# Modulating x and context by pairs of channel chunks, with a new order of loads and products and unread products while x arrives

## The chip, the cores and the metric

The kernel runs on one core of a Trainium2 chip. The metric is the device time of one execution in microseconds. Before the change it is 1221.16 us, the median of three runs (1216.76, 1221.16 and 1223.71). The engines are named as the profile names them: PE (TensorE, with PEld for its weight loads), ACT (ScalarE), DVE (VectorE), POOL (GpSimd) and SP (SyncE, which here only issues DMAs).

## The reference, cut to what matters

One layer of a trunk with three token mixers and a mixture of experts. The change touches only what stands in front of the mixers: the normalised input is scaled and shifted per channel ("modulated") and multiplied by the columns of `w_in`. x has 512 tokens, the context 256, and both have 1024 channels.

```python
def rms_norm(x, g):                      # float32: x * rsqrt(mean(x*x) + EPS) * g
def modulate(h, shift, scale):
    return h * (1 + scale[:, None, :]) + shift[:, None, :]
# shift, scale = columns 0..1023 and 1024..2047 of  silu(c) @ w_mod + b_mod
# (c for x, c_ctx for the context);  h = rms_norm(x, g_mix)
px = split_columns(hx @ w_in)            # hx: modulated x, hc: modulated context
pc = split_columns(hc @ w_in)            # retention, window, neighbourhood attention, gates follow
...
# router, 16 experts of 64 tokens each, final norm
```

## The kernel before

Tokens are turned so that channels lie on the 128 partitions; there are eight chunks `k` of 128 channels. A modulated chunk is kept as two float32r tiles, a rounded part ("hi", `hx0h`) and the rest ("lo", `hx0l`; a tile `hx0` holds chunks 0 and 1, `hx1` holds 2 and 3, and so on; `hc0` and `hc1` hold four context chunks each). A product with 128 columns of `w_in` is three matmuls on each chunk: hi by hi, hi by lo, lo by hi (`quantum`). A "unit" is one such product over all eight chunks, and a pump (`Pump`) runs the many units of the kernel one after another between the mixers' own work.

`start()` builds the modulated chunks and runs the first two units meanwhile: those of v and k of the first retention head. Their weights come as tiles `rw` and are split by `halves` into `wv` and `wk`. Their sums for x lie in the PSUM banks `px` and `om`, those for the context in two banks named `oc`. For each chunk these steps follow one another:

- `load_mod(k)`: two DMAs of 512 KB of `w_mod` into `wm` (128 columns of shift and 128 of scale for all 1024 channels of c, so 512 bytes to a piece).
- `mod_rows`: 16 matmuls on 32 columns of PE each give shift and scale as rows; ACT copies them to `rm`.
- `mod_cols`: two matmuls with `rm` as weights turn them into columns; DVE adds the bias (`modT`) and makes the factor (`am`).
- `turn_x`, `turn_c`: PE transposes of the normalised rows `xs` (four tiles of x, two of the context) into one of the rotating PSUM banks `pa`.
- `modulate`: ACT writes hi, then DVE (for the context ACT) the full value `tf`, then DVE subtracts for lo.
- `prod`: the three matmuls of both units, for x (512 columns) and for the context (256).

`row_stat` has ACT square each row tile (`junk`) with a sum, and DVE and POOL make the factor `rstd` of it; `row_norm` applies it on DVE. `pinned[0] = True` holds every engine to the order in which `start()` is written. In that order the rows of chunk k+2, the columns and the modulation of chunk k+1 and the products of chunk k stand beside one another. SP issues DMAs in program order, each on one of eight semaphores, so a DMA waits for the landing of the eighth before it. Behind `start()` the units and the mixers follow, then routing, then 16 experts whose weights (201 MB) are streamed through the buffers that come free.

Of the kernel before, what the change touches and what calls it, by code (L numbers as in the profile page):

```python
# [8 lines left out]
F32 = mybir.dt.float32  # L9
# [40 lines left out]
def kernel(ctx, tc, x, c, cctx_x, c_ctx, w_mod, b_mod, g_mix, g_ffn, w_in, decay, ret_gn, w_ret,  # L50
# [74 lines left out]

    def split(hi, lo, src):
        A.activation(hi, src, AF.Copy)
        V.tensor_tensor(lo, src, f32(hi), op=OP.subtract)
# [15 lines left out]
            [(sink_b, dap(sink, 0, [[0, P], [1, HW]]))]]  # L144
    xs = []
    for i in range(4):
        xs.append(Tp.tile([P, D], F32, name="xs", tag="t"))
        SY.dma_start(xs[i], dap(x, i * P * D, [[D, P], [1, D]]))
        for dst, src in vecs[i]:
            SY.dma_start(dst, src)  # L150
    ident = cs[:, C_ID:C_ID + P]
# [49 lines left out]
    NM = 6 * D  # L201
# [25 lines left out]
    def load_mod(k):  # L227
        ts = []
        for part in range(2):
            t = Tp.tile([P, KT, P], F32, name="wm", tag="t")  # L230
            SY.dma_start(t, dap(w_mod, part * D + k * P, [[NM, P], [P * NM, KT], [1, P]]))  # L231
            ts.append(t)
        return ts

    def mod_rows(wt):
        o = px()
        for part in range(2):
            for k2 in range(2):
# [7 lines left out]
    def mod_cols(k, rm):  # L246
        o = px()
        for j in range(2):
            mm(o[:, 2 * j:2 * j + 2], rm[:, j * P:(j + 1) * P], sel2, True, True)
        b_ = colv[:, 16:32].rearrange("p (a k) -> p a k", a=2)[:, :, k:k + 1]  # L250
        V.tensor_tensor(modT[:, :, k, :], o[:, 0:4].rearrange("p (a n) -> p a n", a=2), b_.to_broadcast([P, 2, 2]),
                        op=OP.add)
        V.tensor_scalar(am[:, k, :], modT[:, 1, k, :], 1.0, colv[:, 32 + k:33 + k], op0=OP.add, op1=OP.mult)
# [7 lines left out]
    def turn_c(k):  # L261
        o = pa()
        for t in range(2):
            PE.transpose(o[:, t * P:(t + 1) * P], xs[4 + t][:, k * P:(k + 1) * P], ident)
        return o[:, :CTX]
# [434 lines left out]
    def start():  # L700
        us = [r0[0], r0[2]]
        wm = [load_mod(0)]
        raw = [us[0].load()]
# [4 lines left out]
        raw.append(us[1].load())  # L708
        wm.append(load_mod(2))
        wm.append(load_mod(3))  # L710
# [14 lines left out]
        def mod_x(k, o):  # L725
            modulate(HX(k), HX(k, 1), o, k, 0)

        def mod_c(k, o):
            modulate(HC(k), HC(k, 1), o, k, 1)
# [3 lines left out]
        for i in (0, 2):  # L733
            row_stat(i, i + 2)
            row_norm(i, i + 2, 0)
        ox, oc, rm = {}, {}, {}
        wsp = []

# [6 lines left out]
        def rows_of(k):  # L745
            rm[k] = mod_rows(wm[k])
            if k < 4:
                wm.append(load_mod(k + 4))

        rows_of(0)  # L750
        ox[0] = turn_x(0)
        if HV == 0:
            wsp.append(halves(raw[0], "wv", V))
        mod_cols(0, rm[0])
        if HV == 1:
            wsp.append(halves(raw[0], "wv", V))
        mod_x(0, ox[0])
        ox[1] = turn_x(1)
        if HV == 2:
            wsp.append(halves(raw[0], "wv", V))  # L760
        rows_of(1)
        mod_cols(1, rm[1])
        prod(0, 0, c=False)
        mod_x(1, ox[1])
        wsp.append(halves(raw[1], "wk", G))
        row_stat(4, 6)
        prod(0, 1, c=False)
        row_norm(4, 6, 0)
        rows_of(2)
        prod(1, 0, c=False)  # L770
        mod_cols(2, rm[2])
        ox[2] = turn_x(2)
        prod(1, 1, c=False)
        oc[0] = turn_c(0)
        mod_c(0, oc[0])
        mod_x(2, ox[2])
        oc[1] = turn_c(1)
        mod_c(1, oc[1])
        rows_of(3)
        for i in range(2):  # L780
            prod(i, 0, x=False)
        oc[2] = turn_c(2)
        mod_c(2, oc[2])
        for i in range(2):
            prod(i, 1, x=False)
        ox[3] = turn_x(3)
        row_norm(0, 6, 1)
        rope_table(0)
        pump.prime()
        for k in range(2, KT):  # L790
            tick(T0)
            if k < 7:
                mod_cols(k + 1, rm[k + 1])
                tick(T1)
                mod_x(k + 1, ox[k + 1])
                tick(T2)
            for i in range(2):
                prod(i, k, c=False)
            if k < 7:
                oc[k + 1] = turn_c(k + 1)  # L800
                mod_c(k + 1, oc[k + 1])
                tick(T3)
            if k < 6:
                rows_of(k + 2)
            for i in range(2):
                prod(i, k, x=False)
            if k < 6:
                ox[k + 2] = turn_x(k + 2)
            if k == 5:
# [934 lines left out]
```

## Time and profile before

| | us |
|---|---|
| runs | 1216.76, 1221.16, 1223.71 |
| profiled execution | 1221.08 |
| its span, first to last instruction | 1219.3 |
| PE busy | 1155.5 (95% of the span) |
| DVE busy | 617.3 (51%) |
| ACT busy | 403.9 (33%) |

The page's chain of work that ended last is 62% PE and 25% DMA (the experts' weights), 7% DVE. A page of the profile shows busy shares over the whole span; what `start()` costs is read from the timeline of its first 70 us. A row of the timeline begins with the start and the duration in us; in square brackets stands how long the engine was idle before it and what it was released by.

### The profile page before, as it was taken

Reading aid. Unit: us, or ns where it says so; the run is one execution under the profiler, and the core shown is the slowest. Engines: PE = TensorE matmul, PEld = TensorE weight load, DVE = VectorE, ACT = ScalarE, POOL = GpSimd, SP = SyncE. Lnnn points to the kernel's source line nnn. Section 1 sums busy time; section 2 is a strip of 40 time slices with the busy share of each in tenths; the row PEclk is TensorE's granted clock in tenths of the full one; section 3 lists DMA queues with packets and bytes.
Section 4 is the critical chain, followed back from the end, with each engine's and each line's share of the span. In section 5 each row is a group of like instructions: output and inputs, shape, how many; then the busy total and the mean of one; then the engine's idle time right before and its main releaser. Section 6 shows DMA issues by size and latency. Waiting matters only on the chain.

```text
span 1219.3 us, 15848 instructions
## 1 busy us (share of the span) xinstructions
PE 1155.5 (95%) x5876; PEld 714.0 (59%) x5876; DVE 617.3 (51%) x1380; ACT 403.9 (33%) x779; POOL 87.0 (7%) x150
## 2 busy tenths in 40 slices
PE   4999999999999999999999979999999999999995
PEld 2788888777668887788888744333333323233322
DVE  3687666698867664677646352232332223222213
ACT  4544334576645553232332232112111111111112
POOL 1011211100040220000000000000000000000001
PEclk9999999999999999999999979999999999999998
DMA  9822112111012124887637548999999999999994
GB/s 274 219 87 70 52 52 89 53 36 35 19 52 62 35 61 166 291 268 244 206 103 293 207 173 313 405 409 409 409 409 409 409 409 409 409 409 409 409 409 184
DMA packets 159978, 285.57 MB, mean 234 GB/s; under 512 B 10838, under 2 KB 100250, under 8 KB 159900
## 3 DMA queue, kind: packets, MB, share of 16 engines
q1 hardware_dynamic: 158172, 278.27, 62.6%
q0 software_dynamic: 1152, 4.19, 0.9%
q10 hardware_dynamic: 576, 2.10, 0.4%
q8 instruction: 46, 0.75, 0.3%
q14 instruction: 32, 0.26, 0.1%
HBM read 280.33 MB, written 4.19 MB: 233 GB/s over the span
## 4 chain that ended last, share of the span: by engine, by line
PE 62%; DMA 25%; DVE 7%; ACT 2%; SPq 1%; issue 1%; POOL 1%; DVEq 0%; POOLq 0%; ACTq 0%
PE px L119 26%; DMA rg<-in_w_exp_up_dram 16%; PE pa L67 10%; PE px L67 8%; DMA rg<-in_w_exp_down_dram 8%; PE pa L119 7%; PE PV L119 3%; PE oc L119 3%; PE pa L1041 1%; PE pa L955 1%; DVE ws L295 1%; PE oy L119 1%; DMA wm<-in_w_mod_dram 1%; DVE rt L445 1%; SPq L231 1%
## 5 line engine op out<-in xcount | busy, mean ns | idle before, releaser
L67 PE MATMUL pa<-rg,xe 128*64 128x512 f32 x1024 | 264.5, 609 | 7.3 <-DMA rg<-in_w_exp_up_dram 4.9
L67 PEld LDWEIGHTS pa<-rg,xe 128*64 128x64 f32 x1024 | 72.4, 137 | 155.4 <-issue 108.7
L67 PE MATMUL px<-rg,hid 128*64 128x512 f32 x512 | 120.2, 601 | 10.9 <-DMA rg<-in_w_exp_down_dram 10.2
L295 DVE TENSOR_TENSOR ws<-rw,ws 128x1024 fp32r<-128x1024 f32 x55 | 68.8, 1252 | 55.6 <-PE px L119 34.9
L67 PEld LDWEIGHTS px<-rg,hid 128*64 128x64 f32 x512 | 32.8, 136 | 90.3 <-issue 48.5
L119 PE MATMUL px<-hx0h,ws 128*128 128x512 f32 x224 | 83.3, 401 | 0.0
L119 PE MATMUL px<-hx3h,ws 128*128 128x512 f32 x224 | 83.2, 398 | 0.0
L119 PE MATMUL px<-hx2h,ws 128*128 128x512 f32 x224 | 82.7, 397 | 0.0
L119 PE MATMUL px<-hx1h,ws 128*128 128x512 f32 x224 | 82.6, 398 | 0.0
L67 DVE SCALAR_TENSOR_TENSOR tt<-px,gcol,m 128x512 f32<-128x512 f32 x16 | 12.0, 751 | 127.7 <-PE px L67 127.7
L67 ACT ACTIVATE yy<-tt 64x512 fp32r<-64x512 f32 x32 | 20.1, 628 | 144.6 <-DVE tt L67 144.2
L67 DVE TENSOR_TENSOR acc<-px,acc 128x512 f32<-128x512 f32 x58 | 37.5, 687 | 59.3 <-PE px L67 59.3
L119 PE MATMUL px<-yh,ws 128*128 128x512 f32 x192 | 62.3, 390 | 0.8 <-ACT mod L1165 0.8
L294 ACT ACTIVATE ws<-rw 128x1024 fp32r<-128x1024 f32 x55 | 57.8, 1052 | 6.4 <-DMA rw<-in_w_in_dram 5.9
L911 ACT ACTIVATE Sx<-Sx,nm 128x512 f32<-128x512 f32 (+1 forms) x64 | 47.9, 748 | 34.7 <-DVE nm L947 19.5
L1160 DVE SCALAR_TENSOR_TENSOR mac<-mw,cpad,mac 128x1024 f32<-128x1024 f32 x30 | 38.5, 1283 | 18.9 <-DMA mw<-in_w_mod_dram 16.6
L119 PEld LDWEIGHTS px<-hx3h,ws 128*128 128x128 f32 x224 | 42.1, 189 | 7.9 <-issue 1.1
L119 PEld LDWEIGHTS px<-hx0h,ws 128*128 128x128 f32 x224 | 42.2, 189 | 7.7 <-issue 0.7
L119 PEld LDWEIGHTS px<-hx2h,ws 128*128 128x128 f32 x224 | 42.6, 190 | 7.1 <-issue 0.2
L119 PEld LDWEIGHTS px<-hx1h,ws 128*128 128x128 f32 x224 | 42.2, 188 | 7.2
L67 ACT ACTIVATE gu<-pa 128x512 f32<-128x512 f32 x16 | 9.5, 596 | 110.1 <-PE pa L67 110.1
L67 DVE TENSOR_SCALAR xe<-px,af,sf 128x128 f32<-128x128 f32 (+1 forms) x36 | 14.0, 403 | 61.1 <-ACT xe L67 41.8
(432 smaller groups left out, 2158.2 us busy)
## 6 DMA issues: line engine op xcount, KB each, us to landing
rg<-in_w_exp_gate_dram SPq DMA_DIRECT2D x128, 512.0 KB, 10.2
rg<-in_w_exp_up_dram SPq DMA_DIRECT2D x128, 512.0 KB, 10.2
rg<-in_w_exp_down_dram SPq DMA_DIRECT2D x128, 512.0 KB, 10.2
rw<-in_w_in_dram SPq DMA_DIRECT2D x58, 512.0 KB, 3.8
mw<-in_w_mod_dram SPq DMA_DIRECT2D x32, 512.0 KB, 4.8
wm<-in_w_mod_dram SPq DMA_DIRECT2D x16, 512.0 KB, 7.4
rw<-in_w_out_dram SPq DMA_DIRECT2D x8, 512.0 KB, 3.6
xs<-in_x_dram SPq DMA_DIRECT2D x4, 512.0 KB, 4.2
```

The costliest lines, as they stand in the source:

```text
L67: return (lambda *a_, **k_: tc.keep_in_program_order(f(*a_, **k_))) if pinned[0] else f
L119: PE.matmul(o, lhsT, rhs, start=start, stop=stop)
L231: SY.dma_start(t, dap(w_mod, part * D + k * P, [[NM, P], [P * NM, KT], [1, P]]))
L294: A.activation(hi, raw, AF.Copy)
L295: V.tensor_tensor(lo[:, :NV], raw[:, :NV], f32(hi[:, :NV]), op=OP.subtract)
L445: V.tensor_copy(t2[b:b + q], o[c:c + q])
L911: A.activation(Sx[:, :n], Sx[:, :n], AF.Exp, scale=-1.0, bias=nm, accum_out=l[:, 0:1])
L955: PE.transpose(o[:, j * P:(j + 1) * P], SXs[b, j][:, ti * P:(ti + 1) * P], ident)
L1041: PE.transpose(o[:, b * P:(b + 1) * P], SXs[a, b][:, ti * P:(ti + 1) * P], ident)
L1160: V.scalar_tensor_tensor(macs[w], tiles[i], cpad[:, k, 0:1], macs[w], op0=OP.mult, op1=OP.add)
```

## The change

- `load_mod(j)` loads the shift and scale of two chunks at once: four DMAs of 512 KB, 256 columns each (1 KB to a piece). The first four are issued right behind x, then both units' weights (`rw`), then the next four, then the context, then the last eight as their buffers come free.
- `mod_rows` and `mod_cols` work on pairs: 16 matmuls of 256 columns, then four with `rm`.
- Columns, modulation and products of a pair follow its rows directly. The context's first two pairs are both modulated in the round of the second x pair.
- The context's statistics and the rest of the normalisation stand ahead of the loop over pairs; the lo part of `wk` is made by DVE instead of POOL.
- `Warm`: eleven matmuls whose result nothing reads: for each tile of x one of 8 columns that reads the tile, and two of 256 columns on constants; two more behind the first pair's columns. They write the bank of the first unit, whose first real product starts it anew.

```diff
+    class Warm:
+        def __call__(self, dep=None, n=1):
+            if dep is not None:
+                k = dep.shape[0]
+                mm(self.o[:, :dep.shape[1]], ident[0:k, :], dep, True, True)
+            for _ in range(n):
+                mm(self.o[:, 0:256], ident, cs[:, 0:256], True, True)
...
+    def load_mod(j):
+        ts = []
+        for part in range(2):
+            for h in range(2):
+                t = Tp.tile([P, 4, 256], F32, name="wm", tag="t")
+                SY.dma_start(t, dap(w_mod, 4 * h * P * NM + part * D + j * 256, [[NM, P], [P * NM, 4], [1, 256]]))
+                ts.append(t)
+        return ts
...
     def mod_rows(wt):
...
                 for g in range(4):
-                    mm(o[32 * g:32 * g + 32, P * part:P * part + P], cpad[:, 4 * k2 + g, :],
-                       wt[part][:, 4 * k2 + g, :], k2 == 0, k2 == 1)
-        rm = h2(name="rm", shape=(P, 2 * P))
-        A.activation(rm, o[:, 0:2 * P], AF.Copy)
+                    mm(o[32 * g:32 * g + 32, 256 * part:256 * part + 256], cpad[:, 4 * h + g, :], wt[2 * part + h][:, g, :],
+                       h == 0, h == 1)
+        rm = h2(name="rm")
+        A.activation(rm, o, AF.Copy)
...
+        warm = Warm(om[0][0])
+        for i in range(4):
+            warm(xs[i][:, 0:8], 2)
         for i in (0, 2):
             row_stat(i, i + 2)
             row_norm(i, i + 2, 0)
...
+        rm = mod_rows(wm[0])
+        wm.append(load_mod(2))
+        ox[0], ox[1] = turn_x(0), turn_x(1)
+        mod_cols(0, rm)
+        wsp.append(halves(raw[0], "wv", V))
+        warm(n=2)
+        mod_x(0)
         prod(0, 0, c=False)
+        mod_x(1)
+        wsp.append(halves(raw[1], "wk", V))
+        prod(0, 1, c=False)
+        ox[2] = turn_x(2)
+        prod(1, 0, c=False)
+        prod(1, 1, c=False)
+        ox[3] = turn_x(3)
+        row_norm(0, 4, 1)
         row_stat(4, 6)
         row_norm(4, 6, 0)
+        row_norm(4, 6, 1)
+        for j in range(1, 4):
+            k = 2 * j
+            rm = mod_rows(wm[j])
+            if j == 1:
+                wm.append(load_mod(3))
+            if j == 2:
+                rope_table(0)
+                pump.prime()
+            mod_cols(j, rm)
+            mod_x(k)
+            kc = 0 if j == 1 else k
+            oc[kc], oc[kc + 1] = turn_c(kc)
+            prod(0, k, c=False)
+            prod(1, k, c=False)
+            mod_x(k + 1)
+            if j < 3:
                 ox[k + 2] = turn_x(k + 2)
+            prod(0, k + 1, c=False)
+            prod(1, k + 1, c=False)
+            while kc <= k:
+                for i_ in range(2):
+                    mod_c(kc + i_)
+                    tick(2)
...
+                for i_ in range(2):
+                    for i in range(2):
+                        prod(i, kc + i_, x=False)
+                kc += 2
+                if kc <= k:
+                    oc[kc], oc[kc + 1] = turn_c(kc)
+            if j < 3:
+                ox[k + 3] = turn_x(k + 3)
+            tick(6)
```

How the instructions stand now. In the PE's row before, in the middle of the loop, stand the rows of chunk 5 (`px<-wm,cpad`), the context's products of chunk 3 (`oc<-`), x turned for chunk 5 (`pa<-cs,xs`), the columns of chunk 5 (`px<-cs,rm`) and the first x product of chunk 4 (`hx2h`):

```order
L67 MATMUL px<-wm,cpad 32x128 x16
L67 MATMUL oc<-hc0h,wv 128x256
L67 MATMUL oc<-hc0l,wv 128x256
L67 MATMUL oc<-hc0h,wv 128x256
L67 MATMUL oc<-hc0h,wk 128x256
L67 MATMUL oc<-hc0l,wk 128x256
L67 MATMUL oc<-hc0h,wk 128x256
L67 MATMUL pa<-cs,xs 128x128 x4
L67 MATMUL px<-cs,rm 128x2 x2
L67 MATMUL px<-hx2h,wv 128x512
```

Now, in the round of chunks 4 and 5, the rows, the columns, the turned context and the x products that need them follow one another:

```order
L67 MATMUL px<-wm,cpad 32x256 x16
L67 MATMUL px<-cs,rm 128x2 x4
L67 MATMUL pa<-cs,xs 128x128 x4
L67 MATMUL px<-hx2h,wv 128x512
L67 MATMUL px<-hx2l,wv 128x512
L67 MATMUL px<-hx2h,wv 128x512
```

So the work that stood between a chunk's rows, its columns and its products has moved behind them.

On ACT, around the context's two squares (`junk`), the row before has the copy of a chunk's rows behind them and then context and x chunks in turn, and two copies of rows (`rm`) ahead:

```order
L67 ACTIVATE rm<-px 128x256
L67 ACTIVATE hx0h<-pa,modT,am 128x512
L67 ACTIVATE wk<-rw 128x512 x2
L67 ACTIVATE junk,ssq<-xs 128x1024 x2
L67 ACTIVATE rm<-px 128x256
```

Now the second pair's copy `rm` stands behind the squares, and both its chunks (`hx1h`) behind it:

```order
L67 ACTIVATE hx0h<-pa,modT,am 128x512 x2
L67 ACTIVATE wk<-rw 128x512 x2
L67 ACTIVATE junk,ssq<-xs 128x1024 x2
L67 ACTIVATE rm<-px 128x512
L67 ACTIVATE hx1h<-pa,modT,am 128x512 x2
```

So ACT reaches chunks 2 and 3 of x only when the context has landed and been squared; before, context chunk 0 and x chunk 2 stood there. On SP the loads stood in this order behind x:

```order
L231 DMA wm<-in_w_mod_dram 128x8x128 x2
L289 DMA rw<-in_w_in_dram 128x8x128
L231 DMA wm<-in_w_mod_dram 128x8x128 x2
L707 DMA xs<-in_ctx_dram 128x1024 x2
L289 DMA rw<-in_w_in_dram 128x8x128
L231 DMA wm<-in_w_mod_dram 128x8x128 x12
```

and now in this:

```order
L165 DMA wm<-in_w_mod_dram 128x4x256 x4
L309 DMA rw<-in_w_in_dram 128x8x128 x2
L165 DMA wm<-in_w_mod_dram 128x4x256 x4
L727 DMA xs<-in_ctx_dram 128x1024 x2
L165 DMA wm<-in_w_mod_dram 128x4x256 x8
```

The context has moved from behind five DMAs of 512 KB (without x) to behind ten. Behind the first retention head all five engines have the same instructions in the same order as before.

## Rows read from the trace of the kernel before

**Rows 1.** Windows: span of each stretch, busy us by engine, granted clock, DMA share, GB/s.
```profile
20.00:40.00 20.00, 16.99 (x144) 11.83 (x136) 8.89 (x22) 9.45 (x18) 4.05 (x4) 1.00 1.08 300
40.00:60.00 20.00, 19.36 (x227) 16.32 (x226) 15.10 (x52) 10.84 (x20) 0.00 (x0) 1.00 0.76 194
60.00:110.00 50.00, 49.26 (x250) 40.51 (x249) 38.26 (x72) 22.31 (x34) 8.59 (x9) 1.00 0.26 74
720.00:740.00 20.00, 17.70 (x70) 10.23 (x72) 6.29 (x32) 3.50 (x12) 1.22 (x1) 0.56 0.33 113
780.00:800.00 20.00, 20.00 (x96) 7.44 (x94) 6.45 (x14) 3.80 (x7) 0.00 (x0) 1.00 1.03 409
```

**Rows 2.** Timeline of PE in `start()`: start, us, what, [idle before, releaser].
```profile
31.26 0.63 PE L67 MATMUL om<-hx0l,wk 128*128 128x512 f32 x1
31.69 0.63 PE L67 MATMUL om<-hx0h,wk 128*128 128x512 f32 x1
...
40.63 0.40 PE L67 MATMUL px<-hx1l,wv 128*128 128x512 f32 x1
40.86 0.39 PE L67 MATMUL px<-hx1h,wv 128*128 128x512 f32 x1
```

**Rows 3.** Timeline of PE, two rounds of the loop at full rate.
```profile
44.72 0.63 PE L67 MATMUL pa<-cs,xs 128*128 128x128 f32 x4 [0.64 <-DVE tf L67]
45.18 0.51 PE L67 MATMUL px<-cs,rm 128*128 128x2 f32 x4
...
54.00 0.51 PE L67 MATMUL px<-cs,rm 128*128 128x2 f32 x4
```

**Rows 4.** Windows with source L119: the pump's matmuls up to the end of `start()`.
```profile
61.00:67.55 6.55, 4.66 (x19) 1.00 0.82 241
```

**Rows 5.** Timeline of PE and ACT where `start()` first uses a landed load.
```profile
14.40 1.08 PE L67 MATMUL px<-wm,cpad 128*32 128x128 f32 x16 [4.22 <-DVE xs L67]
...
26.28 1.15 ACT L67 ACTIVATE wk<-rw 128x512 fp32r<-128x512 f32 x2 [1.24 <-DMA rw<-in_w_in_dram]
```

**Rows 6.** DMA totals, of 35 to 41 us and of 800 to 860 us.
```profile
DMA packets 3445, 1.75 MB, mean 291 GB/s; under 512 B 52, under 2 KB 3444, under 8 KB 3444
```
```profile
DMA packets 6733, 24.55 MB, mean 409 GB/s; under 512 B 748, under 2 KB 748, under 8 KB 6730
```

**Rows 7.** Timeline, the context's statistics: the second square and the first normalisation.
```profile
28.38 1.04 ACT L67 ACTIVATE junk<-xs 128x1024 f32<-128x1024 f32 x1
...
31.58 0.88 DVE L67 TENSOR_SCALAR xs<-xs,rstd 128x512 f32<-128x512 f32 x2
```

**Rows 8.** Timeline, from a chunk's columns to its product with lo.
```profile
22.74 1.02 PE L67 MATMUL px<-cs,rm 128*128 128x2 f32 x4 [0.51 <-ACT rm L67]
...
24.26 0.78 ACT L67 ACTIVATE hx0h<-pa,modT,am 128x512 fp32r<-128x512 f32 x1 [1.57 <-DVE am L67]
...
25.07 0.81 DVE L67 TENSOR_SCALAR tf<-pa,am,modT 128x512 f32<-128x512 f32 x1 [0.85 <-ACT hx0h L67]
...
25.92 0.69 DVE L67 TENSOR_TENSOR hx0l<-tf,hx0h 128x512 fp32r<-128x512 f32 x1
...
26.66 0.80 PE L67 MATMUL px<-hx0l,wv 128*128 128x512 f32 x1 [0.78 <-DVE hx0l L67]
```

**Rows 9.** Timeline at full rate: rows, their copy, a context chunk, a copy of 512 columns.
```profile
47.32 1.08 PE L67 MATMUL px<-wm,cpad 128*32 128x128 f32 x32
...
47.48 0.56 ACT L67 ACTIVATE hc1h<-pa,modT,am 128x256 fp32r<-128x256 f32 x1
...
48.53 0.39 ACT L67 ACTIVATE rm<-px 128x256 f32<-128x256 f32 x1
...
66.69 0.58 ACT L477 ACTIVATE vt<-px 128x512 f32<-128x512 f32 x1
```

**Rows 10.** Windows: PE empty, and PE just after it had work again.
```profile
232.50:235.40 2.90, 0.00 (x0) 0.00 (x0) 2.83 (x5) 1.26 (x2) 1.22 (x1) 1.00 0.00 0
236.00:239.00 3.00, 3.00 (x11) 2.52 (x10) 2.77 (x8) 1.47 (x3) 0.00 (x0) 0.50 0.58 171
```

More of the change, by code (lines that the diff above doesn't have):

```diff
@@ L150 @@
             SY.dma_start(dst, src)
+    wmod0.append(load_mod(0))
     ident = cs[:, C_ID:C_ID + P]
@@ L225, in row_norm @@
             E.tensor_scalar(v, v, rstd[:, i:i + 1], None, op0=OP.mult)
[L227 to L233, printed above, removed]
     def mod_rows(wt):
@@ L237, in mod_rows, with mod_cols @@
         for part in range(2):
-            for k2 in range(2):
+            for h in range(2):
                 for g in range(4):
-                    mm(o[32 * g:32 * g + 32, P * part:P * part + P], cpad[:, 4 * k2 + g, :],
-                       wt[part][:, 4 * k2 + g, :], k2 == 0, k2 == 1)
-        rm = h2(name="rm", shape=(P, 2 * P))
-        A.activation(rm, o[:, 0:2 * P], AF.Copy)
+                    mm(o[32 * g:32 * g + 32, 256 * part:256 * part + 256], cpad[:, 4 * h + g, :], wt[2 * part + h][:, g, :],
+                       h == 0, h == 1)
+        rm = h2(name="rm")
+        A.activation(rm, o, AF.Copy)
         return rm
-    def mod_cols(k, rm):
+    def mod_cols(j, rm):
         o = px()
[L248 to L253, printed above, removed]
+        for c_ in range(4):
+            mm(o[:, 2 * c_:2 * c_ + 2], rm[:, c_ * P:(c_ + 1) * P], sel2, True, True)
+        ks = slice(2 * j, 2 * j + 2)
+        b_ = colv[:, 16:32].rearrange("p (a k) -> p a k", a=2)[:, :, ks]
+        V.tensor_tensor(modT[:, :, ks, :], o[:, 0:8].rearrange("p (a k n) -> p a k n", a=2, n=2),
+                        b_[:, :, :, None].to_broadcast([P, 2, 2, 2]), op=OP.add)
+        V.scalar_tensor_tensor(am[:, ks, :], modT[:, 1, ks, :], 1.0,
+                               colv[:, 32 + 2 * j:34 + 2 * j][:, :, None].to_broadcast([P, 2, 2]), op0=OP.add, op1=OP.mult)
     def turn_x(k):
@@ L262, in turn_c @@
         o = pa()
-        for t in range(2):
-            PE.transpose(o[:, t * P:(t + 1) * P], xs[4 + t][:, k * P:(k + 1) * P], ident)
-        return o[:, :CTX]
+        for i in range(2):
+            for t in range(2):
+                PE.transpose(o[:, i * CTX + t * P:i * CTX + (t + 1) * P], xs[4 + t][:, (k + i) * P:(k + i + 1) * P], ident)
+        return o[:, :CTX], o[:, CTX:]
     def modulate(hi, lo, o, k, who):
@@ L701, in start @@
         us = [r0[0], r0[2]]
-        wm = [load_mod(0)]
-        raw = [us[0].load()]
+        wm = wmod0
+        raw = [u.load() for u in us]
         wm.append(load_mod(1))
@@ L723, in prod, with mod_x, mod_c @@
             us[i].quantum(k % 4, w, om[i][0] if x else None, om[i][1] if c else None, k=k)
[L725 to L729, printed above, removed]
+        def mod_x(k):
+            modulate(HX(k), HX(k, 1), ox.pop(k), k, 0)
+        def mod_c(k):
+            modulate(HC(k), HC(k, 1), oc.pop(k), k, 1)
         om = [(px(), OC()[:, :CTX]), (pa("om"), pa("oc")[:, :CTX])]
         pinned[0] = True
[L733 to L737, printed above, removed]
         dg = decays()
@@ L743, in tick @@
                 next(dg, None)
[L745 to L761, printed above, removed]
@@ L774, in start @@
[L774 to L807, printed above, removed]
-                ox[k + 2] = turn_x(k + 2)
-            if k == 5:
-                pump.prime2()
+        row_norm(4, 6, 1)
@@ new lines, in start @@
+        for j in range(1, 4):
[14 more added lines that the diff above has]
+            if j < 3:
+                ox[k + 2] = turn_x(k + 2)
+            prod(0, k + 1, c=False)
[4 more added lines that the diff above has]
+                    tick(2)
+                if j == 3:
+                    pump.prime2()
+                for i_ in range(2):
+                    for i in range(2):
+                        prod(i, kc + i_, x=False)
[5 more added lines that the diff above has]
+            tick(6)
```

21 lines of the change are left out of this document (8 added, 13 removed).

## Prediction

> **What bounds the kernel now.** I read the windows first. Between 20 and 110 us PE is busy 16.99 of 20, 19.36 of 20 and 49.26 of 50 us [rows 1], so from about 40 us on a microsecond of delay in `start()` is a microsecond for PE, and the mixers behind it are PE's too. The experts' loads do not swallow it: from 780 us on they run at 409 GB/s, but from 720 to 740 us at 113 GB/s [rows 1], with their buffers full until PE uses the first of them; their long run begins when PE gets there. I therefore count a shift at the end of `start()` in full.
>
> The timeline of PE in `start()` gives its two speeds. At 31 us two matmuls of 512 columns start 0.43 us apart, at 40 us 0.23 us apart [rows 2]: half rate (1.2 GHz) and full rate (2.4 GHz). The change in speed lies between, at about 34 us. The rounds of the loop at full rate show how tight the present order is: from the columns at 45.18 to those at 54.00 two chunks pass, 4.41 us each, with one wait of 0.64 us just ahead [rows 3]. The last product of `start()` ends at about 67.5 us, but 19 matmuls of the pump stand among its last ones [rows 4]; at 0.23 us they are 4.3 us. Without them `start()` ends at 63.2 us. That is the number to beat.
>
> **The change, step by step.** I give times on the axis of the profile of before, and add up what PE waits for in its new row.
>
> *The loads.* Before, PE uses the first `wm` tile at 14.4 us, and ACT gets the second unit's weights, seven DMAs later, at 26.28 [rows 5]: 7 x 0.524 MB in 11.9 us, 308 GB/s. Those pieces are of 512 bytes (291 GB/s when nothing else runs); pieces of 4 KB run at 409 [rows 6]. For the 1 KB pieces of the new `wm` tiles no row stands alone, so their rate lies between 291 and 409; I take the middle, 350, or 1.5 us for a DMA, with 1.7 for `rw` and 1.3 for the context. In the new order the context ends eleven DMAs behind the first `wm`: 7 x 1.5 + 2 x 1.7 + 2 x 1.3 = 16.5, so at 14.3 + 16.5 = 30.8 us. The ends are 14.3 + 11 x 1.28 = 28.4 and 14.3 + 11 x 1.80 = 34.1.
>
> The Trainium skill ("DMA: Bandwidth & Descriptors", section "Why small descriptors are slow") puts a fixed overhead of about three beats of 32 bytes on each packet. By that estimate 1 KB gains 9% on 512 bytes, not 20%, and the context would land about a microsecond later; no row here shows it.
>
> *Up to the rows of the second pair.* The unread matmuls fill PE while x lands, and I let them lift it to full rate before the first `wm` is used, instead of at 34 us. This buys little by itself, for what follows waits for loads and for ACT and DVE. The first pair's last `wm` lands at 14.3 + 3 x 1.5 = 18.8, `rw` at 20.5; ACT splits it in 1.15 [rows 5] and makes hi in 0.8 [rows 8], to 22.5; DVE is then still at the second of two subtractions of 0.69, to 23.0, and gives a lo every 1.5 (0.81 + 0.69 [rows 8]), the second at 26.1. Behind it PE has the rest of chunk 1, a turned chunk, six matmuls of the second unit and a turned chunk, 2.9, to 29; the second pair's rows end at 30.8.
>
> *The context's statistics ahead of the second pair.* ACT copies the second pair's rows only behind both squares, DVE adds its bias only behind the context's normalisation. From the start of the second square to the first normalisation pass 3.2 us, and a pair of normalisations takes 0.88 [rows 7]; there are two pairs. So 30.8 + 3.2 + 1.8 = 35.8 us until DVE reaches the second pair. From the end of the columns (23.76) to ACT's hi (24.26) pass 0.5 us, from there to the product with lo (26.66) 2.4 [rows 8]. PE goes on at 35.8 + 0.5 + 2.4 = 38.7 us. Since 30.8 it has had only some columns and one turned pair to do. Before, at this time, it has done nearly the same work (the x products of two chunks, the context's of one or two, the rows of four). So up to here the change gains and loses nothing.
>
> *The three rounds.* What a round adds is the line rows, copy, columns, modulation, in which PE now has nothing else to do. At full rate, for a pair: the rows take 1.8 us (32 records of 128 columns take 1.08, twice the columns somewhat less than twice that); the copy of 512 columns 0.13 + 0.58 [rows 9]; four column matmuls 0.85 (two take 0.51 with their tail [rows 3]); then 0.5 and 2.4 as above. That is 6.3 us until lo is there. The rest: five matmuls at 0.23, 1.1; a turned chunk 0.5 (0.63 with its tail [rows 3]); six matmuls of the second chunk 1.4 (its lo is ready 1.5 after the first's, just in time); the context's twelve of 256 columns, at half of 0.23, 1.4; a turned chunk 0.5: 4.9. A round takes 11.2 us where two chunks took 8.8.
>
> - The round of chunks 2 and 3, from 38.7: 4.3 for x and the first context pair; then the second context pair, which is turned and modulated with PE waiting: 0.5, four ACT operations of 0.56 [rows 9] less overlap and a subtraction 2.5, the last matmuls 0.6, a turned chunk 0.5. To 47.1.
> - The round of chunks 4 and 5: 11.2, to 58.3.
> - The round of chunks 6 and 7, without turned chunks: 6.3 + 1.1 + 0.3 + 1.4 + 1.4 = 10.5, to 68.8.
>
> Against 63.2 this is 5.6 us later, at full rate throughout.
>
> *The clock.* PE has 8 us nearly without work before 38.7. A stall of 2.9 us with nothing in it was followed by a granted clock of 0.50 while PE worked through (236 to 239 us) [rows 10], a wait of 0.64 us was not [rows 3]. So full rate is lost there; the row shows 3 us of work at half, I take 4 with its edges, which cost 2 us. The rounds of chunks 4 and 5 and of 6 and 7 have each a wait of 0.7 us and, since the turned context needs a bank that DVE's `tf` frees, one of 2.1 us (0.5 + 0.78 + 0.81). The nearer row, 2.9, says that the rate falls; I take it for one of the two rounds, 2 us, and keep 0 and 4 as ends.
>
> *What moves out of `start()`.* The pump's first splits of weights now stand behind DVE's work for the two units; before, three stood ahead. PE has 11 us of pump work per two units there, so I take 0.5 us (0 to 2.4, two subtractions of 1.2). The `wk` lo on DVE instead of POOL, and SP's later loads (rope, the pump's weights), lie inside the waits above.
>
> Sum: 5.6 + 2 + 2 + 0.5 = 10 us. The durations are of the profiled execution, 1221.08 us (span 1219.3 and 1.8 around it), which is within 0.1 us of the median of the runs. Forecast: 1231 us, 0.8% slower.
>
> **Rivals.**
>
> *The clock holds.* If the waits in the later rounds and the one at 30 us do not cost full rate, or the columns and turned chunks in them keep it up, only 5.6 us and less remain; with the context at 28.4 us instead of 30.8 it is 3 us. For it speaks that waits of half a microsecond are harmless; against it rows 10. 1224 to 1227 us.
>
> *Faster: PE at full rate from 15 us is what counts.* Of PE's 17 us of work between 20 and 40 us [rows 1] the most runs at half rate, which the unread matmuls could spare. If PE's waits in the rounds were covered, the loads alone would set the end: the last `wm` lands 15 x 1.5 + 3.4 + 2.6 = 28.5 us after the first, at 42.8; the last pair needs 9.3 us more, so 52.1, 11 us ahead of 63.2, 1210 us. It decides at one point: whether the x products of chunk 2 run by about 32 us. Against it stand the rows of ACT, in which the copy waits for the context, and of PE, in which no other products stand between a pair's rows and its modulation.
>
> *Much slower: each wait costs the clock.* The Trainium skill ("TensorE: Matmul & The Clock Gate", section "HAM oscillation") describes bursts of matmuls with waits between, each of which starts at half rate anew. As a mechanism here: the fall at 30 us, both later rounds, and the second context pair's wait, 2 us each, with the context at 34.1: 5.6 + 8 + 3.3 + 0.5 = 17 us, 1238 us. No row shows the clock behind a wait of about 2 us.
>
> *The unread products do nothing.* If they do not lift the rate, the rows of the second pair end some 2 us later than the context's statistics allow; it adds at most 2 us to the forecast, and stays inside it.
>
> **The numbers.** The forecast with its neighbours (7 to 14 us slower, the fourth rival in it) gets 0.53, the holding clock 0.26, the much slower case 0.12, the faster 0.09. A difference under 0.5% (6 us) can hardly be told from none in this kernel, whose runs of before lie 7 us apart. Slower by more than that: nearly all of the forecast, the much slower case and little of the holding clock, 0.66; within it 0.25; faster 0.09. The range leaves out the faster case and the worst: 1220 to 1239 us.
>
> **What would show it.** Right: the first 512-column matmuls near 22 us 0.23 us apart; PE nearly idle between 31 and 38 us, put down to ACT and DVE; its granted clock 0.50, or matmuls 0.43 apart, just behind it; rounds of about 11 us; the first pump matmul near 70 us; the rest shifted by the same amount. Wrong: the x products of chunk 2 before 34 us, rounds under 9.5 us, or a shift at 70 us that is gone at 230.

## The result and the profile after

| | median of runs, us | ratio to before (95% interval) | span of the profiled run, us |
|---|---|---|---|
| before | 1221.08 (1216.76 to 1223.71, 4 runs) | | 1219.3 |
| after | 1231.89 (1231.48 to 1238.55, 4 runs) | 1.0119 (1.0098 to 1.0141) | 1229.7 |

The change makes the kernel slower, as forecast, and the median is 0.9 us from the forecast time. The ratio, 1.2%, is not the quotient of the two medians, which is 0.9% (10.8 us): the one run of 1238.55 weighs in it. The time is lost where the prediction looked for it. The first four stretches of [rows 1], the last moved by 11 us since the work in it is (busy us of PE, PEld, DVE, ACT and POOL, granted clock, DMA share, GB/s):

```profile
20.00:40.00 20.00, 13.69 (x80) 9.20 (x79) 12.60 (x29) 9.69 (x17) 1.54 (x2) 0.81 1.09 354
40.00:60.00 20.00, 15.95 (x103) 12.48 (x103) 9.03 (x36) 6.01 (x12) 0.00 (x0) 0.85 0.47 129
60.00:110.00 50.00, 46.60 (x255) 37.73 (x254) 32.51 (x52) 22.83 (x34) 5.15 (x5) 0.97 0.22 64
731.00:751.00 20.00, 16.16 (x72) 9.15 (x74) 7.71 (x37) 4.70 (x14) 1.22 (x1) 0.63 0.32 114
```

PE is busy 3.3 us less from 20 to 40 us, 3.4 less from 40 to 60 and 2.7 less behind that, and the granted clock is below 1.00 in all three. The 1.00 of before in the first stretch is not full rate throughout: up to about 34 us its products of 512 columns start 0.43 us apart [rows 2], while the window shows 1.00 from the first microsecond on. That early in a run the spacing tells the clock, not the window. The loads are faster (354 GB/s where they ran at 300) and over sooner (129 GB/s in the second stretch), which helps little: none of PE's waits below is put down to a load, and one of ACT's is (1.08 us for the context).

The timeline of PE in `start()` shows the waits; its line has start, length, the operation and, in brackets, the idle time before it and what ended it:

```profile
22.17 0.50 PE L67 MATMUL px<-hx0h,wv 128*128 128x512 f32 x1 [0.36 <-ACT hx0h L67]
...
29.91 1.93 PE L67 MATMUL px<-wm,cpad 128*32 128x256 f32 x32
33.16 1.05 PE L67 MATMUL px<-cs,rm 128*128 128x2 f32 x8 [1.31 <-ACT rm L67]
35.24 1.26 PE L67 MATMUL pa<-cs,xs 128*128 128x128 f32 x4 [1.03 <-DVE xs L67]
37.51 0.80 PE L67 MATMUL px<-hx1h,wv 128*128 128x512 f32 x1 [1.00 <-ACT hx1h L67]
39.08 0.80 PE L67 MATMUL px<-hx1l,wv 128*128 128x512 f32 x1 [0.78 <-DVE hx1l L67]
...
49.61 1.93 PE L67 MATMUL px<-wm,cpad 128*32 128x256 f32 x32
52.26 1.05 PE L67 MATMUL px<-cs,rm 128*128 128x2 f32 x8 [0.72 <-ACT rm L67]
55.43 0.66 PE L67 MATMUL pa<-cs,xs 128*128 128x128 f32 x4 [2.11 <-DVE tf L67]
...
62.80 1.93 PE L67 MATMUL px<-wm,cpad 128*32 128x256 f32 x32
65.45 1.05 PE L67 MATMUL px<-cs,rm 128*128 128x2 f32 x8 [0.72 <-ACT rm L67]
68.71 0.63 PE L67 MATMUL pa<-cs,xs 128*128 128x128 f32 x4 [2.20 <-DVE tf L67]
...
74.98 0.40 PE L119 MATMUL px<-hx0h,ws 128*128 128x512 f32 x1
```

Each pair of chunks has the same line: rows (`px<-wm,cpad`), a wait of 0.72 us for their copy, the columns (`px<-cs,rm`), a wait of 2.1 to 2.2 us until VectorE's `tf` gives a bank for the turned context. The first pump matmul, with all products of `start()` ahead of it, is at 74.98 us; the number to beat was 63.2. So the start is 11.8 us longer.

What held the second pair stands in the timelines of ACT and DVE:

```profile
31.47 1.06 ACT L67 ACTIVATE junk<-xs 128x1024 f32<-128x1024 f32 x1 [1.08 <-DMA xs<-in_ctx_dram]
32.53 0.58 ACT L67 ACTIVATE rm<-px 128x512 f32<-128x512 f32 x1
36.68 1.45 ACT L67 ACTIVATE hx1h<-pa,modT,am 128x512 fp32r<-128x512 f32 x2 [3.57 <-DVE am L67]
```
```profile
34.70 1.68 DVE L67 TENSOR_SCALAR xs<-xs,rstd 128x512 f32<-128x512 f32 x4
36.29 0.16 DVE L67 TENSOR_TENSOR modT<-px,colv 128x8 f32<-128x8 f32 x1
```

The copy `rm` stands behind the context's second square, and the bias of the columns (`modT`) behind the context's normalisation.

The windows show four stretches at 1.2 GHz, each behind waits (the clock is the third number from the end), and full rate between them:

```profile
25.50:28.80 3.30, 3.30 (x10) 2.71 (x11) 2.63 (x6) 0.00 (x0) 0.00 (x0) 0.50 1.06 390
...
35.80:42.50 6.70, 4.92 (x14) 3.42 (x14) 4.79 (x14) 3.27 (x6) 0.00 (x0) 0.50 1.10 356
42.60:56.10 13.50, 9.45 (x83) 7.24 (x81) 3.90 (x16) 4.07 (x8) 0.00 (x0) 1.00 0.49 121
56.20:59.60 3.40, 3.40 (x11) 2.81 (x11) 3.16 (x12) 1.86 (x4) 0.00 (x0) 0.50 0.00 0
59.70:69.80 10.10, 7.18 (x69) 5.60 (x68) 2.62 (x7) 2.47 (x4) 0.34 (x1) 1.00 0.00 0
69.90:73.20 3.30, 3.30 (x9) 2.58 (x8) 1.96 (x8) 2.79 (x6) 0.85 (x2) 0.50 0.00 0
```

PE is busy for 14.9 us at half rate there. Before, `start()` ran at half rate up to 34 us, and from there on there was no such stretch.

Behind the start the shift can be followed at waits that both kernels have. At 235.47 us PE waits for `yn` before, at 247.48 after: 12.0 us. At the routing and at the end the traces read, before and then after:

```profile
713.80 0.61 PE L67 MATMUL oc<-cs,affp 128*64 128x128 f32 x2 [2.39 <-DVE affp L67]
...
749.89 1.10 PE L67 MATMUL px<-ohs,acc 128*128 128x64 f32 x8
...
1206.81 0.61 PE L67 MATMUL oc<-yy,OT 128*128 128x512 f32 x2
```
```profile
726.33 0.61 PE L67 MATMUL oc<-cs,affp 128*64 128x128 f32 x2 [2.73 <-DVE affp L67]
...
760.31 1.10 PE L67 MATMUL px<-ohs,acc 128*128 128x64 f32 x8
...
1217.28 0.61 PE L67 MATMUL oc<-yy,OT 128*128 128x512 f32 x2
```

The shift is 12.5 us at the first line, 10.4 at the second and 10.5 at the last. Between the first two the clock is at half rate in both kernels, for 23.9 us before and 20.5 after; 3.4 us less at half rate would be 1.7 us of the 2.1 that come back (an estimate: half of 3.4, PE taken as busy).

### The profile page after: what moved, and what is told of

Read it like the earlier page. It is cut to its first block, busy times and chain, and to the rows that moved or that the text cites. A ratio compares the mean times of both kernels' runs of the same rounds, so it can differ in the third digit from the quotient of the medians.

```text
span 1229.7 us, 15621 instructions
## 1 busy us (share of the span) xinstructions
PE 1160.3 (94%) x5776; PEld 717.5 (58%) x5776; DVE 617.3 (50%) x1374; ACT 403.2 (33%) x775; POOL 84.2 (7%) x148
## 3 DMA queue, kind: packets, MB, share of 16 engines
q1 hardware_dynamic: 149980, 278.27, 61.5%
## 4 chain that ended last, share of the span: by engine, by line
PE 64%; DMA 23%; DVE 8%; ACT 2%; issue 1%; POOL 1%; SPq 0%; DVEq 0%; POOLq 0%; ACTq 0%
PE px L119 25%; DMA rg<-in_w_exp_up_dram 12%; PE pa L67 12%; PE px L67 9%; DMA rg<-in_w_exp_down_dram 7%; PE pa L119 7%; PE PV L119 3%; PE oc L119 3%; DMA wm<-in_w_mod_dram 2%; PE pa L1047 1%; PE pa L961 1%; DVE ws L315 1%; PE oy L119 1%; DMA rw<-in_w_out_dram 1%; DVE rt L465 1%
## 5 line engine op out<-in xcount | busy, mean ns | idle before, releaser
L67 PE MATMUL px<-rg,hid 128*64 128x512 f32 x512 | 120.4, 601 | 11.7 <-DMA rg<-in_w_exp_down_dram 11.0
L119 PE MATMUL px<-hx0h,ws 128*128 128x512 f32 x224 | 83.5, 401 | 0.0
L119 PE MATMUL px<-hx3h,ws 128*128 128x512 f32 x224 | 83.2, 398 | 0.0
L119 PE MATMUL px<-hx1h,ws 128*128 128x512 f32 x224 | 83.0, 398 | 0.0
L119 PE MATMUL px<-hx2h,ws 128*128 128x512 f32 x224 | 82.5, 396 | 0.0
L119 PE MATMUL px<-yh,ws 128*128 128x512 f32 x192 | 62.2, 390 | 0.0
L119 PEld LDWEIGHTS px<-hx3h,ws 128*128 128x128 f32 x224 | 42.2, 189 | 8.0 <-issue 1.1
L119 PEld LDWEIGHTS px<-hx0h,ws 128*128 128x128 f32 x224 | 42.2, 189 | 7.7 <-issue 0.7
L119 PEld LDWEIGHTS px<-hx2h,ws 128*128 128x128 f32 x224 | 42.6, 190 | 6.9
L119 PEld LDWEIGHTS px<-hx1h,ws 128*128 128x128 f32 x224 | 42.3, 189 | 7.1
L119 PE MATMUL px<-hx1l,ws 128*128 128x512 f32 x112 | 44.9, 400 | 0.0
```

What stands on the lines that cost most here:

```text
L67: return (lambda *a_, **k_: tc.keep_in_program_order(f(*a_, **k_))) if pinned[0] else f
L119: PE.matmul(o, lhsT, rhs, start=start, stop=stop)
```

## The experiments

The ratios are to runs of the kernel before on the same chip; its median was 1218.87 us beside e1 to e4, 1217.74 beside e5 to e8, 1217.57 beside e9 and 1218.04 beside e10 to e12. "Start" is the first pump matmul: 74.98 after; for the kernel before the end without the pump's share, 63.2, compares. Each start is read from one profiled run, and the same code of `start()` came at 74.98 (after) and 78.45 (e12), and at 59.91 (e9) and 61.31 (e10). So a difference of up to some 3 us between two starts is not shown by the starts alone. Against the 1.0119 of after, the intervals of e3 to e11 lie clear below; those of e1, e2 and e12 overlap it.

| kernel | median, us | ratio (95%) | start, us |
|---|---|---|---|
| e1, after without unread products | 1231.68 | 1.0091 (1.0057 to 1.0126) | 75.07 |
| e2, after, context loaded first | 1229.92 | 1.0083 (1.0053 to 1.0113) | 73.45 |
| e3, after, waits of the rounds filled | 1225.44 | 1.0054 (1.0034 to 1.0074) | 70.15 |
| e4, after, rows ahead | 1223.47 | 1.0035 (1.0016 to 1.0054) | 66.61 |
| e5, e4 and context first | 1221.87 | 1.0026 (1.0014 to 1.0038) | 66.19 |
| e6, before with unread products | 1219.50 | 1.0019 (1.0004 to 1.0034) | |
| e7, e4, statistics behind | 1221.01 | 1.0020 (1.0009 to 1.0031) | 67.54 |
| e8, e7 with two waits filled | 1219.69 | 1.0018 (1.0005 to 1.0032) | 64.37 |
| e9, e8, last pair early | 1219.52 | 1.0005 (0.9990 to 1.0020) | 59.91 |
| e10, e9, routing filled | 1213.01 | 0.9955 (0.9940 to 0.9971) | 61.31 |
| e11, before, routing filled | 1214.14 | 0.9963 (0.9951 to 0.9975) | |
| e12, after, routing filled | 1228.69 | 1.0083 (1.0066 to 1.0101) | 78.45 |

**e1, the unread products left out.** They are fourteen, not the eleven told ahead: three for each of four tiles of x and two behind the first pair's columns.

```
-        warm = Warm(om[0][0])
-        for i in range(4):
-            warm(xs[i][:, 0:8], 2)
...
-        warm(n=2)
```

> The changed kernel without its eleven unread products. Theory (the line rows, copy, columns, modulation and the late context set the time, the early full rate buys little): the second pair's rows end up to 2 us later at half rate, all else is the same, so 1232 to 1234 us; PE's first 512-column products start 0.43 us apart. Rival (the unread products carry the start, and without them the change would be much worse): 5 us or more above the changed kernel, 1237 us and up.

The start moved by 0.1 us, and no difference in time is shown (1231.68 us, just under the 1232 to 1234 of the theory). Without them the clock still became full, at 32.4 us instead of 15.2, and fell later, at 39.2; the second pair's first product with lo is at 39.21 us against 39.08. No gain from the unread products of this change is to be seen: what follows them waits for ACT, DVE and loads.

**e2, the context's two loads ahead of the second pair's four.**

```
-        wm.append(load_mod(1))
         for i in range(2):
             ...
             SY.dma_start(xs[4 + i], dap(cctx_x, i * P * D, [[D, P], [1, D]]))
+        wm.append(load_mod(1))
```

> The changed kernel with the context's two loads issued ahead of the second pair's four. Theory (the copy of the second pair's rows waits for the context): the context lands some 5 us earlier, PE reaches the first product with lo of chunk 2 at about 36.4 us instead of 39.1, and the whole is 2 to 4 us faster than the changed kernel, 1228 to 1230 us. Rival (the second pair's own loads set this point): they land 2.6 us later, so no gain or a loss of 1 to 2 us, 1232 to 1234 us.

The median came out as in the theory (1229.92 us), but the interval overlaps that of after. The start came 1.5 us earlier, less than the 2 to 4 of the theory, because the rival takes part of it: the second pair's last tile is now the late one. The half-rate stretches behind it are as long as after's (6.8, 3.4 and 3.4 us), so the 1.5 us are not the clock's.

```profile
32.18 0.64 PE L67 MATMUL px<-wm,cpad 128*32 128x256 f32 x8 [1.41 <-DMA wm<-in_w_mod_dram]
...
37.73 0.79 PE L67 MATMUL px<-hx1l,wv 128*128 128x512 f32 x1 [0.78 <-DVE hx1l L67]
```

**e3, unread products in the waits of the rounds.**

```
             mod_cols(j, rm)
+            Warm(px())(n=3 if j == 1 else 4)
             mod_x(k)
```

(and behind the rows, 3 or 1, and behind the second pair's turned context, 3)

> The changed kernel with further unread products on constants in the waits of the three rounds (behind a pair's rows, its columns, and in the first round behind the turned context). The waits stay, PE only works in them. Theory (three stretches at half rate, 3.4 to 6.8 us each, cost about 5 us of the 11): granted clock 1.00 from 15 us on or with one short fall, 4 to 6 us faster than the changed kernel, 1226 to 1228 us. Rival (the half rate hides in the waits, only the waits themselves cost): no change, 1231 to 1233 us.

The clock stayed full from 26.9 us to the end of the start, and the start came 4.8 us earlier:

```profile
26.90:40.00 13.10, 11.41 (x80) 8.12 (x80) 6.75 (x18) 6.05 (x11) 1.54 (x2) 1.00 1.08 359
40.00:55.00 15.00, 13.35 (x102) 10.11 (x101) 5.91 (x23) 4.73 (x10) 0.00 (x0) 1.00 0.67 180
55.00:70.00 15.00, 14.57 (x107) 11.35 (x106) 8.36 (x28) 7.35 (x13) 1.29 (x2) 1.00 0.00 1
```

The chain through ACT and DVE that each round waits for is the same as after; only what PE does meanwhile differs. From a round's rows to its columns pass 2.7 us in both, from the columns to the turned context 3.1 (after 3.2 to 3.3), so the added products hold nothing up. The rounds themselves:

```profile
38.87 0.49 PE L67 MATMUL px<-hx1l,wv 128*128 128x512 f32 x1 [1.07 <-DVE hx1l L67]
...
47.80 1.93 PE L67 MATMUL px<-wm,cpad 128*32 128x256 f32 x32
...
59.42 1.93 PE L67 MATMUL px<-wm,cpad 128*32 128x256 f32 x32
```

From the first product with lo of chunk 2 to the next rows 8.9 us pass, then 11.6 to the last rows and 10.7 to the pump; after these are 10.5, 13.2 and 12.2. Each round lost 1.5 to 1.6 us by the clock, 4.6 us of the 4.8. So some 4.8 of the 11.8 us are shown to be the clock's, and the median bears it out (1225.44 us, just under the 1226 to 1228 of the theory).

**e4, rows, columns and first modulation of the next pair between the products of this one.**

```
+        rm = mod_rows(wm[1])
...
         for j in range(1, 4):
...
             prod(1, k, c=False)
...
             if j < 3:
+                rm = mod_rows(wm[j + 1])
                 ox[k + 2] = turn_x(k + 2)
             prod(0, k + 1, c=False)
             prod(1, k + 1, c=False)
...
+                mod_cols(j + 1, rm)
...
+                mod_x(k + 2)
```

> The changed kernel with the rows and columns of the next pair and its first modulation moved ahead, between the products of the present pair; loads, pairs and unread products as they are. Theory (each of the rounds of chunks 4 to 7 pays 2.4 us for its line, and their waits of 2 us cost the clock twice): rounds of about 8.5 us instead of 11 to 13, 7 to 9 us faster than the changed kernel, 1223 to 1225 us. Rival (the loads of pairs, landing late, set the rounds): no more than 2 us gained, 1230 us and up.

The edit also moves the turned context and its modulation ahead of the pair's x products. The median is as the theory said (1223.47 us). The long waits of the two later rounds are gone (0.28 and 1.07 us are left in the last) and with them two of the half-rate stretches: 8.4 us earlier at the start. These 8.4 us hold the clock of the later rounds, so they and the 4.8 of e3 must not be added. Besides the early one at 27 us one half-rate stretch stayed, behind the second pair's waits, with the third pair's rows in it at 3.47 us instead of 1.93:

```profile
38.13 0.79 PE L67 MATMUL px<-hx1l,wv 128*128 128x512 f32 x1 [1.04 <-DVE hx1l L67]
...
40.56 3.47 PE L67 MATMUL px<-wm,cpad 128*32 128x256 f32 x32
```

This is the main cause, shown by taking it away: the rounds of the change put each pair's chain through ACT and DVE where PE has no other products to do.

**e5, e4 with the edit of e2.**

> The version with rows, columns and first modulation of the next pair moved ahead, with the two context rows loaded ahead of the second pair's four quarter tiles. Theory (the context's landing still sets the start of the second pair's products, as in the version with that edit alone, where it gave 1.5 us): first low-half product of chunk 2 at 36.5 us instead of 38.1, first pumped product at 65.1 instead of 66.6, 1222 us. Rival (with the rows ahead of the loop, the second pair's own weights, later by the same edit, come last): that product at 38 or later, first pumped product at 66.3 or later, 1223 to 1224 us.

0.4 us at the start, and unclear by itself. The context's squares are over at 27.8 us instead of 31.7, and from the first product with lo of chunk 0 to that of chunk 2 pass 11.9 us instead of 13.8 (25.90 to 37.83; in e4 24.38 to 38.13): the theory's gain. But ahead of all that the first modulation waited 1.66 us for its `am`, where in e4 it waited 0.41. The columns ahead of it took 1.71 us instead of 0.95, for the clock had fallen at 19.3 us (in e4 at 26.7). Whether that belongs to the edit or to the run stays open.

**e6, the unread products alone, in the kernel before.**

```
+        warm = Warm(om[0][0])
+        for i in range(4):
+            warm(xs[i][:, 0:8], 2)
         for i in (0, 2):
             row_stat(i, i + 2)
```

> The kernel before, in its own order and with its own loads, with the unread products on the arriving x alone added in front of its first rows. Theory (before 34 us PE is not the bound: loads, ScalarE and VectorE are): the granted clock is full from about 14 us, the products get shorter, and the end of the start moves by less than 0.7 us; 1218 to 1220 us, the same as before. Rival (the half-rate stretch up to 34 us is what holds the start): of the some 14 us that PE is busy between 14 and 34 us at half rate it gets back 3 us or more; the end of the start 3 us earlier, 1216 us or less.

The theory holds at its upper end, and the interval leaves a loss of 0.04 to 0.34%. The clock is full from 15.2 us, yet the rounds begin 0.5 us later than before (the rows of [rows 9] at 47.81 us, where they stood at 47.32), and by 26 us it has fallen again, until 35.7:

```profile
26.00:30.00 4.00, 2.34 (x26) 1.17 (x29) 0.17 (x1) 3.23 (x6) 2.96 (x3) 0.50 1.13 286
```

So these products gave a full clock for 10 us only, and what one held up to 34 us would be worth is not shown.

**e7, e4 with the context's statistics and normalisation behind the second pair's columns and modulations, and its first turned chunks behind that pair's x products.**

```
+        mod_cols(1, rm)
+        mod_x(2)
+        mod_x(3)
         row_stat(4, 6)
         row_norm(4, 6, 0)
+        row_norm(0, 4, 1)
         row_norm(4, 6, 1)
```

> Rows, columns and first modulations ahead, and the context's statistics and normalization moved on VectorE and ScalarE behind the second pair's columns and its two modulations; the context's turned chunks behind the second pair's four x products. Theory (VectorE's context statistics stand in front of the second pair's columns and hold PE): the first low-half product of chunk 2 at 35.5 to 36.2 us instead of 38.1, the third pair's rows at 39 to 40 instead of 40.6, the first pumped product at 64 to 65 instead of 66.6, 1221 to 1222 us. Rival (the wait is only moved: the context's turned chunks come 2 us or more late behind the x products): PE waits at the first turned context chunk, first pumped product at 66 or later, 1223 us or more.

Each came true in part. From the first product with lo (25.21 us; 24.38 in e4) to that of chunk 2 pass 12.0 us instead of 13.8, so the statistics had held PE; from there to the pump 30.4 instead of 28.5. The first context pair is now turned in that time, and PE waits 0.65 us for the second one's modulation, where e4 had no wait:

```profile
37.18 0.79 PE L67 MATMUL px<-hx1l,wv 128*128 128x512 f32 x1 [0.89 <-DVE hx1l L67]
...
49.45 0.38 PE L67 MATMUL oc<-hc0h,wv 128*128 128x256 f32 x1 [0.65 <-ACT hc0h L67]
```

The median is 2.5 us below that of e4 all the same; the batches are two, and the ratios (1.0020 and 1.0035) overlap. No gain or loss of e7 over e4 is shown.

**e8, e7 with three unread products behind the second pair's rows and three behind its columns.**

> The version before this one with three more unread products in each of the two waits of the second pair (behind its rows and behind its columns). Theory (the one half-rate stretch that is left comes from those waits): no half-rate record between 30 and 66 us, the third pair's rows in 1.93 us instead of 3.47, the first pumped product 1.5 to 2.5 us earlier than in the version without them, 62 to 63 us, and 1219 to 1220 us, level with the kernel before. Rival (the clock falls all the same or a little later, and the products only delay the columns): the first pumped product within 0.5 us of that version, or later, 1221 to 1223 us.

The clock is full from 30 us on, the rows take 1.93 us, and the start ends 3.2 us earlier than in e7; 1.3 of these stand already at the first product with lo (23.91 us), ahead of the edit, so 1.9 are its own, within the 1.5 to 2.5 expected (the 62 to 63 us named for the start were not reached):

```profile
37.86 1.93 PE L67 MATMUL px<-wm,cpad 128*32 128x256 f32 x32
```

By time no gain of e8 over e7 is shown: 1.0018 and 1.0020.

**e9, e8 with the last pair's rows in a wait of the context, and each chunk of x modulated a round ahead.**

```
                 oc[2], oc[3] = turn_c(2)
...
+                rm = mod_rows(wm[3])
                 mod_x(4)
...
+                ox[6] = turn_x(6)
+                mod_x(6)
```

> The filled version, with the last pair's rows on PE in the wait for the context's second turned chunks (1.19 us of waits in that version), its columns behind it, and each x chunk modulated about one round ahead. Theory (the 3.0 us of waits that are left in the two later rounds come from VectorE and ScalarE getting the last pair's work late, all within 8 us): no wait over 0.5 us behind 48 us, first pumped product at 61.5 to 62.5 us instead of 64.4, 1216.5 to 1218 us, level with the kernel before or up to 1 us faster. Rival (the modulations are only moved to a place where VectorE and ScalarE are as full, and PE waits there instead): first pumped product at 63.8 us or later, 1219 us or more. Either way a kernel faster than before by more than 0.2% is not expected: PE has nearly the same products to do in the start.

The start went past the expected 61.5 us, to 59.91, with PE busy throughout: 3.3 us ahead of the kernel before. The time does not show it (1219.52 us, level with before). At 710 us the lead is still 3.7 us; then the half-rate stretch of the routing lasts 31 us, not 24:

```profile
710.13 0.61 PE L67 MATMUL oc<-cs,affp 128*64 128x128 f32 x2 [2.38 <-DVE affp L67]
...
749.30 1.10 PE L67 MATMUL px<-ohs,acc 128*128 128x64 f32 x8
```

Against the 749.89 us of before 0.6 us is left, and from there to the end both take 457 us. The length of that stretch does not go with the kernel: in the profiled runs it is 17 us in e3, e5, e7 and e8, 20 to 24 in before, after, e1 and e2, and 31 in e4, e6 and e9. So this accounts for the profiled run of e9, not for its median.

**e10, e11, e12: the routing's waits filled, in e9, before and after.**

```
     group_sum(3)
+    Warm()(n=5)
     rsqrt_end(rs2, rv2, TT, V)
```

(likewise 2, 5, 3 and 3 unread products at the next four waits)

> The version with the last pair early, whose lead of 3.7 us at 710 us was 0.6 us behind the half-rate stretch there, with unread products in PE's five waits of the routing stage (710 to 726 us). Theory (the lead is real and was lost in a longer half-rate stretch, 31 us against 24): no half-rate record from 713 to 740 us, the stage some 5 us shorter, and the whole 3 to 4 us ahead of the kernel before with the same fill, about 1210 us, faster than both kernels. Rival (the stage is bound by VectorE's chain of maxima and by the experts' loads, or the fill delays it): 1217 us or more.

> The kernel before with the same unread products in the routing stage alone. Theory (PE's half-rate stretch of 23.9 us behind 713.7 us costs some 5 us of PE work, and the experts' long run starts that much earlier without it): 1212 to 1214 us. Rival (loads or VectorE bound that stage): 1217 to 1219 us, the same as before.

> The changed kernel with the same unread products in the routing stage. Theory (the shift of 12 us at the end of the start goes through in full once the half-rate stretch, 20.5 us here and 23.9 in the kernel before, is out of both): 11.5 to 12.5 us above the kernel before with the same fill, 1224 to 1226 us. Rival (part of the shift is swallowed by the experts' loads): 9 us or less above it.

The window of the routing, of before and of e10, which gets there 1.5 us earlier:

```profile
713.00:725.00 12.00, 5.67 (x18) 1.93 (x18) 9.15 (x39) 4.35 (x14) 0.56 (x2) 0.53 0.56 214
```
```profile
713.00:725.00 12.00, 9.55 (x54) 6.91 (x53) 9.26 (x39) 4.51 (x15) 0.56 (x2) 1.00 0.49 186
```

The half-rate stretch is gone in all three. Before gains 0.37% (0.25 to 0.49), e10 0.45% (0.29 to 0.60): it beats both kernels of the case, though the gain is the routing's. Over e11 it has 1.1 us of the median, less than the runs of e11 differ (1210.67 to 1216.27), and not the 3 to 4 of its theory. e12 lies 14.6 us above e11, neither the 12 of the theory nor the 9 of the rival. But nothing is swallowed by the loads. The routing of e11 and then of e12:

```profile
715.35 0.38 PE L67 MATMUL oc<-cs,affp 128*64 128x128 f32 x2
...
745.29 1.10 PE L67 MATMUL px<-ohs,acc 128*128 128x64 f32 x8
```
```profile
730.44 0.38 PE L67 MATMUL oc<-cs,affp 128*64 128x128 f32 x2 [0.48 <-DVE affp L67]
...
760.40 1.10 PE L67 MATMUL px<-ohs,acc 128*128 128x64 f32 x8
```

Both are 15.1 us apart, and the two profiled times (1216.27 and 1231.27 us) 15.0: with the clock full there, the shift goes through whole. Between the two lines 29.9 to 30.0 us pass in e10, e11 and e12; unfilled it was 33 to 39 us.

The start of e12 was itself longer than after's: 78.45 us, in a profiled run that lay 2.6 us above its median. Of the 3.5 us 1.1 are there at the first product with lo (25.02 us, 23.95 after). The rest comes in the three rounds, whose half-rate stretches are longer (after 6.7, 3.4 and 3.3 us):

```profile
35.50:45.70 10.20, 7.69 (x20) 5.50 (x21) 6.06 (x17) 3.27 (x6) 0.00 (x0) 0.50 1.10 341
56.00:62.70 6.70, 5.26 (x17) 4.38 (x18) 5.29 (x16) 3.14 (x6) 0.00 (x0) 0.50 0.00 0
69.70:76.40 6.70, 4.92 (x14) 4.08 (x15) 4.18 (x10) 4.33 (x7) 1.28 (x2) 0.50 0.00 0
```

Why the same waits cost a longer stretch in one run than in another is open.

## Why the prediction was right, step by step

- *What bounds it.* PE's time in `start()` counts in full: the shift of 11.8 us at 75 us is 12.0 at 247 and 12.5 at 726. Right. The prediction did not see that the routing's clock can change a shift by 2 us and more.
- *Loads.* The 350 GB/s taken for 1 KB pieces was 354 (from 35 to 41 us), with PE and ACT at work beside it:

```profile
DMA packets 2066, 2.12 MB, mean 354 GB/s; under 512 B 64, under 2 KB 2044, under 8 KB 2065
```

  Against the 291 of [rows 6] that is 22% more. The three beats a packet of the Trainium skill ("DMA: Bandwidth & Descriptors", section "Why small descriptors are slow") alone would have given 9%, an estimate from the page; the trace does not agree. The context was awaited until 31.5 us, forecast 30.8.
- *Unread products.* Full rate at 22 us, as said, and of no use (e1). Not foreseen: the rate fell again at 25.5 us, behind waits of 0.4 and 1.3 us.
- *Statistics ahead of the second pair.* PE goes on with lo at 39.08 us, forecast 38.7. The order on ACT and DVE is as told [rows 7]. That they are the only hold is not so: with them moved (e7) the pair's own chain still takes PE to 37.2 us, 12.0 us behind the first product with lo, where after it is 15.1.
- *Rounds.* At full rate 8.4, 11.2 and 10.5 us were forecast. At full rate throughout, in e3, they took 8.9, 11.6 and 10.7. The waits forecast as 0.7 and 2.1 were 0.72 and 2.11 to 2.20. Right to 0.5 us a round, but all three are short, 1.2 us in sum.
- *Clock.* The prediction took 2 us behind 38.7 and 2 us for one of the two later rounds. The rate fell in both. Against e3 the three rounds after took 1.6, 1.6 and 1.5 us more: 4.6 instead of 4. So the price of a fall was taken too high and the number of falls too low. Waits of 0.72 and 2.1 us with the column products (eight records of two columns) between them cost the rate as the 2.9 us of [rows 10] did.
- *Splits moved out.* 0.5 us was taken; the shift is 11.7 us at 120 us, as at 75. No run shows a cost of it.
- *The sum.* 5.6 us forecast at full rate, 1.2 more of it, 4.6 of clock and 0.4 of the second pair's are the 11.8; the forecast was 10. Every term but the splits came out larger. That the time is only 0.9 us from the forecast is partly luck: in the profiled run the routing gave 2.1 us back.
- *The signs.* PE's long idle stretch before 39 us, the clock of 0.50 just behind it and the shift that stays are as named. The first pump matmul "near 70 us" does not follow from the prediction's own sum, 63.2 + 10 = 73.2; it was 74.98. Rounds of "about 11 us" were 10.5, 13.2 and 12.2.
- *The rivals.* The clock did not hold. "PE at full rate from 15 us" fell by its own point: the x products of chunk 2 ran at 39 us, not by 32. "Each wait costs the clock" came true in part: three of the four waits that it names cost full rate, 4.6 us instead of 8. The second context pair's did not (waits of 0.66 and 0.53 us at 46 and 47 us, with the clock at 1.00 from 42.6 to 56.1), and its late context did not come (31.5 us, not 34.1). "The unread products do nothing" did not come about, since they lifted the rate; but leaving them out cost no time (e1).

## What to carry to other kernels

Before chunks are joined into pairs, write down what the engine that bounds the stage will do during one pair's chain through the others; the saving in loads and instructions is nothing if the answer is "wait". Issue the next pair's chain between this pair's products (e4 gave back 8.4 of 11.8 us by order alone, the clock that it kept included). Price a wait of two microseconds on PE as itself and again as the slower work behind it, and put unread products where PE waits with its real work due next, not where it waits for loads anyway (e3 and e11 against e1 and e6).

## What the runs showed that was not expected

- Short waits with work between them went ahead of a fall of the clock: it fell at 25.5 us after waits of 0.36, 1.28 and 0.48 us with products of 512 columns between, and in the later rounds after waits of 0.72 and 2.1 to 2.2 us with the column products between.
- The half-rate stretch of the routing lasted 17 to 31 us in the same instructions, and the routing with the first expert products 33 to 39 us; with its waits filled these took 30 us in three kernels of three. What sets the length is open; unfilled, it makes gains or losses of a few microseconds ahead of it hard to see.
